# A hybrid decoder layer on one core: LayerNorm 1 rows normalised on another engine, and the last two blocks' sums in another order

## The chip, the cores and the metric

The kernel runs on one core of one Trainium2 chip. The metric is the device time of one execution in microseconds (us), lower is better. Engines are named as in the profile: PE (TensorE matmul), PEld (its weight load), DVE (VectorE), ACT (ScalarE), POOL (GpSimd), SP (SyncE, which here issues the DMAs).

## The reference, cut

One layer of a decoder trunk on a residual stream x of 1024 tokens by 1024 channels, in fp32:

```python
h = x * (1 + scale1) + shift1
y = concat(ssd_heads(h), attention_heads(h)) @ W_out
x = layer_norm(alpha * x + (1 + gate1) * y, g1, b1)      # LayerNorm 1
h = x * (1 + scale2) + shift2
x = layer_norm(alpha * x + (1 + gate2) * (relu(h @ W1)**2 @ W2), g2, b2)
```

The change lies at the seam in the middle: the last product of the mixer (`@ W_out`), LayerNorm 1, and the first products of the feed-forward part (`h @ W1`).

## The kernel before

Products of fp32 values are made as three products of split values: every operand is a high part (a cast to fp32r, mostly on ACT, L81) and a low part (raw minus high, mostly on DVE, L85), and PE adds high by high, high by low and low by high.

**The loop over token blocks.** The output projection runs over 8 blocks of 128 tokens (`for tb in range(TB)`, ending at L865). For a block, `out_mm` issues 24 products of 128x512 for each half of the channels, 48 in all; `y_rms` makes the RMS factor of the next block's rows (a product into `rms_ps`, DVE L628, POOL L629); L860 scales a half; and `norm` (L761 to L777) adds the residual (L767), takes the statistics (L768, L769), adds the epsilon (L770), takes the power on POOL (L771) and normalises the 128x1024 row block `u` on DVE (L777). For the last block the row is normalised in two halves, L774 on DVE and L775 on ACT, after a small DVE operation (L773) that makes the bias for ACT.

**To the feed-forward part.** `to_h2` of block tb is called one block later: PE transposes `u` in two halves of four (L813, into a PSUM tile `t_ps` of a tag "S" that has two buffers, shared with `rms_ps`), ACT copies the halves out with scale and bias (L820, four copies a half). The feed-forward products W1 are made in the way of Strassen and Winograd, with seven products of block sums of `h` and W1 instead of eight. Blocks 0 to 3 are split directly into the operands `h_hl`. For blocks 4 to 7 four sums of two token halves are made, t1, t3, t2 and t4 (L795), on POOL for blocks 4 and 5 and on DVE for 6 and 7, and their splits are the operands `h_s`. In the profile `u` is the row block, `h_t` the transposed half (and the tiles of t2 and t3), `h_f` the tiles of t1 and t4, `w_s` and `raw_w` block sums of W1 made on POOL (L792 adds, L795 subtracts), `w_op` their split parts.

**Behind the loop.** The first two column pairs of W1 run the two products that need only blocks 0 to 3 and the low halves (48 matmuls, `f_ps<-h_hl,w_op`, L961). Then their third operand's sums are made (`next(p.w)`), `to_h2` of the last block runs, the sums are split (`h_split` 5, 6, 4, 7), and the other five products follow in the order 5, 6, 4, 7, 3.

**What sets the order.** Each engine runs its instructions strictly in the order in which the build lays them down. The build's scheduler picks that order with a cost model of its own; the code's order and `issue_after` (the kernel's `after`) bound it. So a line that is moved in the code can move other engines' instructions past each other.

## Time and profile before

| | us |
|---|---|
| median of 3 timed runs | 1740.33 (1738.44 to 1745.25) |
| the profiled execution: its own time | 1742.31 |
| the profiled execution: span of the trace | 1740.6 |
| PE busy in the span | 1650.5 (95%) |
| DVE busy | 1235.1 (71%) |
| POOL busy | 820.7 (47%) |
| ACT busy | 763.8 (44%) |

The granted clock of PE is 0.98 over the whole span. The share of an engine is an average over many stages. The seam that the change touches is the stretch from 994 to 1126 us, and it is read from the timelines of the engines there: each row of a timeline has a start, a length, the engine, the line, the operation with its tiles, and in brackets how long the engine had been idle and what released it.

### The profile page before, as it was taken

Reading aid. Unit: us, or ns where it says so; the run is one execution under the profiler, and the core shown is the slowest. Engines: PE = TensorE matmul, PEld = TensorE weight load, DVE = VectorE, ACT = ScalarE, POOL = GpSimd, SP = SyncE. Lnnn points to the kernel's source line nnn. Section 1 sums busy time; section 2 is a strip of 40 time slices with the busy share of each in tenths; the row PEclk is TensorE's granted clock in tenths of the full one; section 3 lists DMA queues with packets and bytes.
Section 4 is the critical chain, followed back from the end, with each engine's and each line's share of the span. In section 5 each row is a group of like instructions: output and inputs, shape, how many; then the busy total and the mean of one; then the engine's idle time right before and its main releaser. Section 6 shows DMA issues by size and latency. Waiting matters only on the chain.

```text
span 1740.6 us, 22970 instructions
## 1 busy us (share of the span) xinstructions
PE 1650.5 (95%) x8316; PEld 1367.9 (79%) x8316; DVE 1235.1 (71%) x1889; ACT 763.8 (44%) x1372; POOL 820.7 (47%) x670
## 2 busy tenths in 40 slices
PE   8999899899999999999899999799999999999996
PEld 6777787788887878888778887688888878888885
DVE  6656677686787777676666378986767865746678
ACT  6557355414444444454565334633333334343322
POOL 4311222256566466354432455566656624705525
PEclk9999999999999999999999999899999999999998
DMA  8134343334444544433323644043444596666512
GB/s 331 37 124 146 109 145 110 121 130 158 154 139 175 165 142 164 138 129 123 121 95 123 228 157 170 37 174 135 146 140 161 172 345 208 250 243 205 193 37 97
DMA packets 112034, 268.73 MB, mean 154 GB/s; under 512 B 10129, under 2 KB 37009, under 8 KB 111921
## 3 DMA queue, kind: packets, MB, share of 16 engines
q1 hardware_dynamic: 111920, 267.27, 44.2%
q8 instruction: 65, 1.06, 0.2%
q14 instruction: 49, 0.39, 0.1%
HBM read 194.22 MB, written 64.62 MB: 149 GB/s over the span
## 4 chain that ended last, share of the span: by engine, by line
PE 63%; DVE 14%; ACT 7%; DMA 6%; POOL 5%; issue 4%; SPq 0%; DVEq 0%; ACTq 0%; POOLq 0%
PE mm_ps L62 20%; PE f_ps L961 15%; PE s_ps L1077 9%; PE y_ps L1077 7%; PE s_ps L62 5%; PE o_ps L62 4%; PE t_ps L550 3%; DVE ada_red L138 2%; DMA w_b<-in_w_dram 2%; ACT scores L421 2%; POOL w_b L186 2%; DMA raw_ada<-in_w_ada_dram 1%; DVE w_hl L85 1%; DVE conv_a L350 1%; POOL raw_ada L136 1%
## 5 line engine op out<-in xcount | busy, mean ns | idle before, releaser
L62 PE MATMUL mm_ps<-h_hl,w_hl 128*128 128x512 f32 x2016 | 506.4, 401 | 10.3 <-POOL w_hl L79 5.6
L62 PEld LDWEIGHTS mm_ps<-h_hl,w_hl 128*128 128x128 f32 x2016 | 375.1, 191 | 88.4 <-POOL w_hl L79 6.5
L85 DVE TENSOR_TENSOR w_op<-raw_w,w_op 128x512 fp32r<-128x512 f32 (+1 forms) x149 | 189.9, 1279 | 22.3 <-ACT w_op L81 21.7
L961 PE MATMUL f_ps<-h_s,w_op 128*128 128x512 f32 x768 | 183.6, 394 | 6.2 <-ACT h_s L81 3.0
L961 PEld LDWEIGHTS f_ps<-h_s,w_op 128*128 128x128 f32 x768 | 145.8, 190 | 38.1 <-ACT h_s L81 3.4
L528 POOL TENSOR_SCALAR probs<-probs,m 128x128 f32<-128x128 f32 (+7 forms) x128 | 103.3, 811 | 123.9 <-DVE m L527 121.7
L81 ACT CAST w_op<-raw_w 128x512 fp32r<-128x512 f32 (+1 forms) x149 | 114.6, 775 | 99.7 <-PE f_ps L961 53.1
L1077 PE MATMUL s_ps<-w_op,a_op 128*128 128x512 f32 x672 | 153.3, 389 | 1.1 <-DVE a_op L85 1.1
L1077 PEld LDWEIGHTS s_ps<-w_op,a_op 128*128 128x128 f32 x672 | 126.0, 188 | 27.8 <-DVE a_op L85 1.6
L85 DVE TENSOR_TENSOR a_op<-a_ld,a_op 128x1024 fp32r<-128x1024 f32 x53 | 79.1, 1494 | 92.3 <-ACT a_op L81 92.3
L526 ACT ACTIVATE probs<-probs,m 128x128 f32<-128x128 f32 (+7 forms) x128 | 99.2, 776 | 100.4 <-DVE m L525 91.1
L961 PE MATMUL f_ps<-h_hl,w_op 128*128 128x512 f32 x576 | 136.8, 389 | 0.0
L79 POOL TENSOR_SCALAR w_hl<-raw_w 128x512 fp32r<-128x512 f32 x86 | 58.8, 685 | 165.1 <-PE mm_ps L62 128.6
L136 POOL TENSOR_TENSOR raw_ada<-raw_ada,c_act 128x1024 f32<-128x1024 f32 x38 | 76.8, 2020 | 126.7 <-DMA raw_ada<-in_w_ada_dram 84.9
L85 DVE TENSOR_TENSOR w_hl<-raw_w,w_hl 128x512 fp32r<-128x512 f32 x88 | 85.5, 974 | 69.5 <-POOL w_hl L79 69.4
L552 ACT CAST pt_hl<-t_ps 128x512 fp32r<-128x512 f32 (+1 forms) x160 | 84.7, 541 | 100.4 <-PE t_ps L550 98.3
L81 ACT CAST a_op<-a_ld 128x1024 fp32r<-128x1024 f32 x53 | 55.7, 1054 | 159.6 <-PE s_ps L1077 80.5
L961 PEld LDWEIGHTS f_ps<-h_hl,w_op 128*128 128x128 f32 x576 | 108.1, 188 | 22.4
L62 PE MATMUL o_ps<-pt_hl,v_s 128*128 128x256 f32 (+1 forms) x640 | 108.9, 295 | 10.2 <-DVE pt_hl L553 4.0
L553 DVE TENSOR_TENSOR pt_hl<-t_ps,pt_hl 128x512 fp32r<-128x512 f32 (+1 forms) x160 | 99.7, 631 | 23.8 <-ACT pt_hl L552 22.3
L1077 PE MATMUL y_ps<-w_op,a_op 128*128 128x512 f32 x504 | 114.7, 389 | 0.0
L523 DVE CUSTOM_DVE_ANT_0 probs<-s_ps,cumrow 128x128 f32<-128x128 f32 (+7 forms) x128 | 94.7, 750 | 25.6 <-PE s_ps L62 18.0
(255 smaller groups left out, 3157.3 us busy)
## 6 DMA issues: line engine op xcount, KB each, us to landing
raw_w<-in_w_dram SPq DMA_DIRECT2D x57, 512.0 KB, 4.1
a_ld<-ad SPq DMA_DIRECT2D x49, 512.0 KB, 4.4
raw_ada<-in_w_ada_dram SPq DMA_DIRECT2D x48, 512.0 KB, 3.6
raw_w<-in_w_in_dram SPq DMA_DIRECT2D x44, 512.0 KB, 3.7
w_b<-in_w_dram SPq DMA_DIRECT2D x14, 1024.0 KB, 7.5
w2t<-w_b SPq DMA_DIRECT2D x14, 1024.0 KB, 4.3
ad<-a_s SPq DMA_DIRECT2D x28, 512.0 KB, 3.4
raw_w<-w2t SPq DMA_DIRECT2D x28, 512.0 KB, 4.8
```

The costliest lines, as they stand in the source:

```text
L62: nc.tensor.matmul(o, l, r, start=start, stop=stop)
L79: nc.gpsimd.tensor_scalar(hi, raw, 1.0, 1.0, op0=ALU.mult, op1=ALU.mult)
L81: nc.scalar.copy(hi, raw)
L85: eng.tensor_tensor(lo, raw, hi.bitcast(F32), op=ALU.subtract)
L136: nc.gpsimd.tensor_tensor(raw, raw, c_act.unsqueeze(2).broadcast_to([P, KT, P]), op=ALU.mult)
L523: nc.vector.tensor_tensor_reduce(out=pt, in0=sp[:, :W], in1=cum[:, :W], op0=ALU.add, op1=ALU.max, scale=1.0, scalar=-3.0e38, accum_out=m[: ...
L526: nc.scalar.activation(pt, pt, AF.Exp, bias=m[:, 1:2], scale=1.0, accum_out=m[:, 2:3])
L528: nc.gpsimd.tensor_scalar(pt, pt, m[:, 3:4], 1.0, op0=ALU.mult, op1=ALU.mult)
L552: nc.scalar.copy(hl[:, 0, :n], tp[:, :n])
L553: nc.vector.tensor_tensor(hl[:, 1, :n], tp[:, :n], hl[:, 0, :n].bitcast(F32), op=ALU.subtract)
L961: nc.tensor.matmul(o, l, r, start=first and k == 0 and m == 0, stop=last and k == 3 and m == 2, skip_group_check=True)
L1077: nc.tensor.matmul(banks[j], ahl[a_][:, n, js], whl[w_][:, n, :], start=first and d == 0 and n == 0 and m == 0, stop=last and d == ND - 1 ...
```

## The change

Three things are changed. First, the rows of LayerNorm 1 for blocks 0 to 6 are normalised by one ACT instruction (L779 of the changed kernel, `u * rstd + bias`), and a small POOL instruction (L778) makes the bias; for the last block the bias comes from POOL too (L773), while the two halves stay on DVE (L774) and ACT (L776). Second, the sums of blocks 4 to 7 are made in the order t1, t2, t4, t3 instead of t1, t3, t2, t4, with t1 right after the first half of the transposes; block 6's copies go to a tile of its own; and the sums of the last two blocks are drawn out between the `h_split` calls. Third, the third operand's sums of W1 for the first two column pairs are held behind the last block's power and DVE half (`after`).

```diff
-        nc.gpsimd.tensor_tensor(mv[:, 3:4], mv[:, 2:3], mhalf[:, 0:1], op=ALU.pow)
+        marks["pow"] = nc.gpsimd.tensor_tensor(mv[:, 3:4], mv[:, 2:3], mhalf[:, 0:1], op=ALU.pow)
         if last:
-            nc.vector.scalar_tensor_tensor(mv[:, 2:3], mv[:, 0:1], -1.0, mv[:, 3:4], op0=ALU.mult, op1=ALU.mult)
-            nc.vector.tensor_scalar(u[:, :512], u[:, :512], mv[:, 0:1], mv[:, 3:4], op0=ALU.subtract, op1=ALU.mult)
+            nc.gpsimd.tensor_scalar(mv[:, 2:3], mv[:, 0:1], mv[:, 3:4], -1.0, op0=ALU.mult, op1=ALU.mult)
+            marks["ln"] = nc.vector.tensor_scalar(u[:, :512], u[:, :512], mv[:, 0:1], mv[:, 3:4], op0=ALU.subtract,
+                                                  op1=ALU.mult)
             nc.scalar.activation(u[:, 512:], u[:, 512:], AF.Identity, bias=mv[:, 2:3], scale=mv[:, 3:4])
         else:
-            nc.vector.tensor_scalar(u, u, mv[:, 0:1], mv[:, 3:4], op0=ALU.subtract, op1=ALU.mult)
+            nc.gpsimd.tensor_scalar(mv[:, 2:3], mv[:, 0:1], mv[:, 3:4], -1.0, op0=ALU.mult, op1=ALU.mult)
+            nc.scalar.activation(u, u, AF.Identity, bias=mv[:, 2:3], scale=mv[:, 3:4])
...
     def to_h2(tb, u):
...
+        both = T4("pt", "h2_t", shape=(P, 2, 4, P)) if tb == TB - 2 else None
...
+            elif both is not None:
+                ht = both[:, hb]
...
+            if tb >= 4 and hb == 0:
+                sub(eng, hf[0][:, :, js], ht, hf[0][:, :, js])
         store(x2d[tb], u)
+        yield
+        if tb < 4:
+            return
+        b12, b22 = hts
+        t1, t4 = hf[0][:, :, js], hf[1][:, :, js]
+        sub(eng, t2f[:, :, js], b22, t1)
+        yield
+        sub(eng, t4, t4, t2f[:, :, js])
+        yield
+        sub(eng, t3f[:, :, js], b22, b12)
+        yield
+        parts(3, b22)
...
-        if before is not None:
-            to_h2(*before)
+        if before is not None and tb < TB - 1:
+            for _ in to_h2(*before):
+                pass
+        elif before is not None:
+
+            with after(marks["ln"]):
+                left = to_h2(*before)
+                next(left)
...
-    for p in first:
-        p.ready.append(next(p.w))
-    to_h2(*before)
+    with after(marks["ln"]), after(marks["pow"]):
+        for p in first:
+            p.ready.append(next(p.w))
+    left = [left, to_h2(*before)]
+    next(left[1])
...
     h_split(5, lambda k: hf[0][:, k, :], ["qk"] * 4)
+    for b in left:
+        next(b)
     h_split(6, lambda k: t2f[:, k, :], ["qk"] * 4)
+    for b in left:
+        next(b)
     h_split(4, lambda k: hf[1][:, k, :], ["v", "v", "w", "w"])
+    for b in left:
+        next(b)
+    for b in left:
+        next(b, None)
     h_split(7, lambda k: t3f[:, k, :], ["pt"] * 4)
```

Since the build lays the order down, what moved is read from the instructions of each engine. In the rows below `u_...` is the row block of one token block (the last one is `u_10002` before and `u_10009` after), `h_t_9242` is t3 and `h_t_9241` t2, and `w_s_10191` and `w_s_10199` before are `w_s_10190` and `w_s_10198` after. Line numbers of the changed kernel are higher by 2 (L795 becomes L797, L792 becomes L794), by 10 to 12 (L813 becomes L823, L820 becomes L832) or by 16 (L843, L844 and L860 become L859, L860 and L876).

POOL before, from the power of block 6 to just behind the power of block 7:

```order
L771 TENSOR_TENSOR mv<-mv,mhalf 128x1
L795 TENSOR_TENSOR w_s_10191<-raw_w 128x512
L792 TENSOR_TENSOR raw_w<-raw_w 128x512
L795 TENSOR_TENSOR h_t_9242<-h_t 128x4x128
L795 TENSOR_TENSOR h_t_9241<-h_t,h_f 128x4x128
L795 TENSOR_TENSOR raw_w<-raw_w 128x512
L795 TENSOR_TENSOR h_f<-h_f,h_t_9241 128x4x128
L795 TENSOR_TENSOR raw_w<-raw_w 128x512
L795 TENSOR_TENSOR w_s_10199<-raw_w 128x512
L792 TENSOR_TENSOR raw_w<-raw_w 128x512
L771 TENSOR_TENSOR mv<-mv,mhalf 128x1
L795 TENSOR_TENSOR raw_w<-raw_w 128x512 x2
```

POOL after, from the power of block 7:

```order
L771 TENSOR_TENSOR mv<-mv,mhalf 128x1
L797 TENSOR_TENSOR w_s_10190<-raw_w 128x512
L797 TENSOR_TENSOR w_s_10198<-raw_w 128x512
L773 TENSOR_SCALAR mv<-mv 128x1
L794 TENSOR_TENSOR raw_w<-raw_w 128x512 x2
L797 TENSOR_TENSOR raw_w<-raw_w 128x512 x4
L797 TENSOR_TENSOR w_s_10515<-raw_w 128x512
```

Before, two sums of W1 stand behind the last power; after, eight do, with the bias of the last block (L773) as the third instruction.

ACT before, from the copies of block 6 to the splits of the last block:

```order
L820 ACTIVATE h_t<-t_ps,b2t,g2t 128x128 x8
L81 CAST h_hl<-h_t 128x2x128 x2
L81 CAST w_op<-raw_w 128x512 x2
L775 ACTIVATE u_10002<-u_10002,mv 128x512
L81 CAST w_op<-raw_w 128x512
L81 CAST w_op<-w_s_10191 128x512
L820 ACTIVATE h_t<-t_ps,b2t,g2t 128x128 x8
L81 CAST h_hl<-h_t 128x2x128
```

ACT after, from the copies of block 5 to those of the last block:

```order
L832 ACTIVATE h_t<-t_ps,b2t,g2t 128x128 x4
L779 ACTIVATE u_9895<-u_9895,mv 128x1024
L832 ACTIVATE h_t<-t_ps,b2t,g2t 128x128 x4
L81 CAST h_hl<-h_t 128x2x128 x2
L81 CAST w_op<-raw_w 128x512
L832 ACTIVATE h_t<-t_ps,b2t,g2t 128x128 x8
L81 CAST h_hl<-h_t 128x2x128 x2
L776 ACTIVATE u_10009<-u_10009,mv 128x512
L81 CAST w_op<-raw_w 128x512 x4
L81 CAST w_op<-w_s_10190 128x512
L832 ACTIVATE h_t<-t_ps,b2t,g2t 128x128 x8
```

The normalisation of block 6 (`L779 u_9895`) stands between the two halves of block 5's copies, as it does for most blocks; and all the casts of W1's third operand (five) stand between the last block's normalisation and its copies, where three of the casts stood ahead of it before.

DVE before, from the last block's normalisation:

```order
L773 SCALAR_TENSOR_TENSOR mv<-mv 128x1
L774 TENSOR_SCALAR u_10002<-u_10002,mv 128x512
L85 TENSOR_TENSOR w_op<-raw_w,w_op 128x512 x3
L85 TENSOR_TENSOR w_op<-w_s_10191,w_op 128x512
L795 TENSOR_TENSOR h_f<-h_t,h_f 128x4x128
L795 TENSOR_TENSOR h_t_9242<-h_t 128x4x128
L795 TENSOR_TENSOR h_t_9241<-h_t,h_f 128x4x128
L85 TENSOR_TENSOR h_hl<-h_t,h_hl 128x2x128
L85 TENSOR_TENSOR h_s<-h_f,h_s 128x512 x2
L795 TENSOR_TENSOR h_f<-h_f,h_t_9241 128x4x128
```

DVE after, from the last block's normalisation:

```order
L774 TENSOR_SCALAR u_10009<-u_10009,mv 128x512
L797 TENSOR_TENSOR h_f<-h_t,h_f 128x4x128
L85 TENSOR_TENSOR h_hl<-h_t,h_hl 128x2x128 x2
L797 TENSOR_TENSOR h_t_9241<-h_t,h_f 128x4x128
L797 TENSOR_TENSOR h_f<-h_f,h_t_9241 128x4x128
L85 TENSOR_TENSOR w_op<-raw_w,w_op 128x512 x4
L85 TENSOR_TENSOR w_op<-w_s_10190,w_op 128x512
L797 TENSOR_TENSOR h_f<-h_t,h_f 128x4x128
L797 TENSOR_TENSOR h_t_9241<-h_t,h_f 128x4x128
L797 TENSOR_TENSOR h_t_9242<-h_t 128x4x128
L85 TENSOR_TENSOR h_hl<-h_t,h_hl 128x2x128
L797 TENSOR_TENSOR h_f<-h_f,h_t_9241 128x4x128
```

Before, only W1's four low parts stood between the last normalisation and the last block's t1; after, block 6's t1, t2 and t4, two of its splits and five low parts stand there. The order on PE and the order of SP's DMAs are the same but for a few matmuls' places.

## Rows read from the trace of the kernel before

**Rows 1.** The page's first part: busy us, share of the span, instructions.

```profile
PE 1650.5 (95%) x8316; PEld 1367.9 (79%) x8316; DVE 1235.1 (71%) x1889; ACT 763.8 (44%) x1372; POOL 820.7 (47%) x670
```

**Rows 2.** Busy us by stretch: PE, PEld, DVE, ACT, POOL (instructions); clock, DMA share, GB/s.

```profile
1065.00:1077.00 12.00, 10.02 (x50) 8.07 (x48) 11.54 (x14) 5.20 (x13) 6.41 (x5) 1.00 0.37 140
1077.00:1089.00 12.00, 10.76 (x53) 8.72 (x52) 11.18 (x14) 4.56 (x12) 9.98 (x7) 1.00 0.34 132
1089.00:1101.00 12.00, 12.00 (x59) 10.03 (x58) 11.20 (x14) 5.12 (x13) 11.24 (x10) 1.00 0.23 87
1101.00:1118.00 17.00, 7.39 (x29) 5.29 (x28) 15.85 (x21) 10.49 (x24) 9.74 (x7) 0.73 0.08 32
1118.00:1150.00 32.00, 32.00 (x132) 26.23 (x133) 28.70 (x43) 16.56 (x32) 10.58 (x8) 0.93 0.26 93
```

**Rows 3.** Timeline of PE, 1062 to 1122 us: start, length, operation, idle before.

```profile
1073.06 0.66 PE L813 MATMUL t_ps<-identf,u 128*128 128x128 f32 x4 [1.04 <-DVE r_rms L628]
...
1079.82 0.63 PE L813 MATMUL t_ps<-identf,u 128*128 128x128 f32 x4
...
1086.42 0.66 PE L813 MATMUL t_ps<-identf,u 128*128 128x128 f32 x4 [1.19 <-DVE r_rms L628]
...
1093.06 1.03 PE L813 MATMUL t_ps<-identf,u 128*128 128x128 f32 x8
1093.85 11.14 PE L961 MATMUL f_ps<-h_hl,w_op 128*128 128x512 f32 x48
1109.22 1.94 PE L813 MATMUL t_ps<-identf,u 128*128 128x128 f32 x8 [4.23 <-DVE u L774]
1114.15 1.22 PE L961 MATMUL f_ps<-h_s,w_op 128*128 128x512 f32 x2 [2.99 <-ACT h_s L81]
```

**Rows 4.** Timeline of PE, 1105 to 1160 us: where PE resumes.

```profile
1117.76 21.16 PE L961 MATMUL f_ps<-h_s,w_op 128*128 128x512 f32 x82 [2.39 <-DVE h_s L85]
```

**Rows 5.** Timeline of DVE, 1062 to 1120 us.

```profile
1065.41 0.81 DVE L777 TENSOR_SCALAR u<-u,mv 128x1024 f32<-128x1024 f32 x1 [0.73 <-POOL mv L771]
...
1090.52 1.77 DVE L777 TENSOR_SCALAR u<-u,mv 128x1024 f32<-128x1024 f32 x1 [0.67 <-POOL mv L771]
...
1104.40 0.14 DVE L770 TENSOR_SCALAR mv<-mv 128x1 f32<-128x1 f32 x1
1104.46 0.68 DVE L795 TENSOR_TENSOR h_t<-h_t,h_f 128x512 f32<-128x512 f32 x1
...
1105.73 1.75 DVE L795 TENSOR_TENSOR h_f<-h_f,h_t 128x512 f32<-128x512 f32 x1
...
1108.54 0.54 DVE L774 TENSOR_SCALAR u<-u,mv 128x512 f32<-128x512 f32 x1
...
1110.80 0.68 DVE L85 TENSOR_TENSOR w_op<-w_s,w_op 128x512 fp32r<-128x512 f32 x1
1111.92 0.69 DVE L795 TENSOR_TENSOR h_f<-h_t,h_f 128x512 f32<-128x512 f32 x1 [0.45 <-ACT h_t L820]
```

**Rows 6.** Timeline of POOL, 1062 to 1120 us.

```profile
1089.94 0.55 POOL L771 TENSOR_TENSOR mv<-mv,mhalf 128x1 f32<-128x1 f32 x1 [0.68 <-DVE mv L770]
...
1100.93 1.30 POOL L795 TENSOR_TENSOR w_s<-raw_w 128x512 f32<-128x512 f32 x1
...
1104.62 0.93 POOL L771 TENSOR_TENSOR mv<-mv,mhalf 128x1 f32<-128x1 f32 x1 [0.69 <-ACT w_op L81]
1105.52 3.08 POOL L795 TENSOR_TENSOR raw_w<-raw_w 128x512 f32<-128x512 f32 x2
```

**Rows 7.** Timeline of ACT, 1062 to 1120 us.

```profile
1071.23 1.06 ACT L619 ACTIVATE y_raw<-y_raw 128x1024 f32<-128x1024 f32 x1 [5.26 <-POOL y_hl L85]
...
1103.96 1.14 ACT L81 CAST w_op<-raw_w 128x512 fp32r<-128x512 f32 x2 [5.33 <-POOL raw_w L792]
1108.65 0.81 ACT L775 ACTIVATE u<-u,mv 128x512 f32<-128x512 f32 x1 [3.55 <-DVE mv L773]
...
1110.40 2.89 ACT L820 ACTIVATE h_t<-t_ps,b2t,g2t 128x128 f32<-128x128 f32 x8
```

More of the change, by code (lines that the diff above doesn't have):

```diff
@@ L807, in to_h2, with parts @@
         eng = nc.vector if tb >= TB - 2 else nc.gpsimd
+        both = T4("pt", "h2_t", shape=(P, 2, 4, P)) if tb == TB - 2 else None
         hts = []
+        def parts(o, ht):
+            for i in range(2):
+                t = hb_hl[o][i]
+                split(ht[:, 2 * i:2 * i + 2, :], t[:, :, 0, js], t[:, :, 1, js], "act")
         for hb in range(2):
@@ L822, in to_h2 @@
             hts.append(ht)
-            o = (1, 2)[hb] if tb < 4 else (None, 3)[hb]
-            if o:
-                for i in range(2):
-                    t = hb_hl[o][i]
-                    split(ht[:, 2 * i:2 * i + 2, :], t[:, :, 0, js], t[:, :, 1, js], "act")
-        if tb >= 4:
-            b12, b22 = hts
-            t1, t4 = hf[0][:, :, js], hf[1][:, :, js]
-            sub(eng, t1, b12, t1)
-            sub(eng, t3f[:, :, js], b22, b12)
-            sub(eng, t2f[:, :, js], b22, t1)
-            sub(eng, t4, t4, t2f[:, :, js])
-        store(x2d[tb], u)
+            if tb < 4:
+                parts(hb + 1, ht)
+            if tb >= 4 and hb == 0:
+                sub(eng, hf[0][:, :, js], ht, hf[0][:, :, js])
+        store(x2d[tb], u)
+        yield
+        if tb < 4:
+            return
[8 more added lines that the diff above has]
+        parts(3, b22)
     def u_pre(tb):
```

## The prediction

> **What bounds the kernel now.** I read the page's first part, then the busy time by stretch around the seam, then the timelines of the four engines there. On the page PE is busy for 1650.5 of 1740.6 us [rows 1], so only the stretches in which PE is idle can give time back. At the seam the stretches say where: PE works 10.02 and 10.76 of 12 us in the last blocks but one, all 12 from 1089 to 1101, 7.39 of 17 from 1101 to 1118, and then all 32 of the next 32 [rows 2]. The reader is to see that DVE is as full as PE in the loop (11.54, 11.18 and 11.20 of 12) and fuller behind it (15.85 of 17), while ACT has more than half of each loop stretch free.
>
> The timeline of PE puts places to this. In the loop PE waits 1.04 and 1.19 us before a second half of transposes, each time for DVE's RMS factor, which stands in DVE's queue [rows 3]. Behind the loop stand the 48 products without a gap, from 1093.85 to 1104.99, and then three waits: 4.23 us for the last block's normalised half (L774), 2.99 for the first split of t1, 2.39 for its low part; PE resumes for good at 1117.76 [rows 3, 4]. These 9.61 us are the large sum at the seam. What ends them is a chain: the last statistics end on DVE at 1104.54 [rows 5], the power on POOL at 1105.55 [rows 6], the last block's t1 starts at 1111.92 [rows 5], and PE resumes 5.84 us after that. So two numbers decide: when the last power is done, and what stands between it and that t1.
>
> **What two engines cost each other.** A DVE sum of 512 columns takes 0.68 us at 1104.46 and 1.75 at 1105.73, where POOL runs sums too; the 1024-wide normalisation takes 0.81 alone and 1.77 beside POOL [rows 5]. Two POOL sums take 3.08 us in that place [rows 6]. Taken as turns this adds up: two POOL sums of 1.24 and one DVE sum of 0.60 are 3.08. One POOL sum with little beside it is 1.30. I take turns as the rule here, 1.24 a POOL sum and 0.60 a DVE operation of 512 with two inputs from SBUF, and keep "no price at all" as the other end.
>
> The Trainium skill (SBUF — State Buffer, "Who interferes with whom") calls the port pair of VectorE and GpSimd an exclusive lock, held for a whole instruction, which a VectorE instruction with two SBUF inputs and a GpSimd one that reads SBUF both need; ScalarE waits for nobody. This speaks for the move of the normalisation to ACT and against the queueing of W1's sums beside the last blocks' sums; rows 5 and 6 agree with it (0.68 against 1.75 us). By the lock alone the tail below comes to the serial sum, 1121.5 for the last t1; by no lock to 1114.8.
>
> **Part 1, the normalisation on ACT.** It takes L777 off DVE, 0.81 to 1.77 us a block [rows 5], seven times. It adds to the chain a small POOL operation, which the trace of before does not show: between nothing and the 0.55 us of the power alone [rows 6], I take 0.4. The ACT instruction is bounded by 1.06 us (a 1024-wide one) and twice 0.81 (the 512-wide one) [rows 7]; I take 1.06. From power to normalised row it is then 1.5 us instead of 0.8 to 1.8, about the same. What changes is the queue: on ACT the normalisation of a block stands ahead of the copies of the previous block's second half, in order. PE's second half for block 5 ends near 1087.1 [rows 3] and its copies could start at once, but they now wait for block 6's power (1090.49) [rows 6] plus 1.5: till 1092.0, then 1.45 for four copies, half of the 2.89 for eight [rows 7]. Behind them wait the splits of that half on DVE, and behind these, in DVE's order, the scaling of the next half; PE's transposes of block 6 need the PSUM buffer that these copies free. Before, those transposes started at 1093.06. Played through with these lengths, block 5's transposes come 1.3 us later than before, its second half 1.6 later, and block 6's 2 to 4 later, so that the 48 products run from about 1097.4 to 1108.5. DVE's gain (1.77 for block 6) and its wait for the splits (about 1.4) nearly cancel: the last power ends at 1105.2 instead of 1105.55. So part 1 gives 0.3 us to the chain, between minus 1.5 and plus 1.5. That the products end 3.5 us later costs nothing as long as the chain behind the power is longer; if it were short, PE could not go on before 1108.5, still 9.3 us before the present 1117.76.
>
> **Part 2 and 3, what stands between the power and the last t1.** On POOL eight W1 sums now stand behind the power where two stood, with the last block's bias as the third instruction. On ACT all five casts of W1's third operand stand between the last normalisation and the last block's copies; the third raw cast needs the fifth of these eight sums. On DVE there stand eleven operations: L774, t1, t2, t4 of block 6, two splits (half as wide, 0.35 each), five low parts.
>
> The whole in turns: eight sums at 1.24 are 9.9, the bias 0.4, DVE 0.45 + 3 x 0.60 + 2 x 0.35 + 5 x 0.60 = 5.95; from 1105.2 that is 1121.5. The last t1 need not wait for the last three POOL sums, so at best with turns it is 3 x 1.24 less, 1117.7. I take 1119.5. Without any price of turns ACT's chain still holds: five sums and the bias, 6.6, to 1111.8; the last three casts 1.6 (two casts of 512 take 1.14); four copies 1.4 [rows 7]: 1114.8. Against 1111.92 before, the last t1 is later by 2.9 at the least, 9.6 at the most, 7.6 in my sum.
>
> **From t1 to PE's resumption** it was 5.84 us. Now t1, t2, t3, one split, t4 stand ahead of the first low part on DVE, 4 x 0.60 + 0.35 + 0.60 = 3.4, with up to two of POOL's sums between (2.5): 3.4 to 5.9, I take 5.4. So PE resumes at 1124.9, between 1118.2 and 1127.4: later by **7.1 us**, 0.4 at the least, 9.6 at the most. After that PE has no idle time that could take it back [rows 2]: the whole lands in the end. The clock is 0.73 in the stretch with the gaps and 0.93 behind it [rows 2]; PE waits before its resumption in both kernels, so I take that cost as equal, plus or minus 1.5. Of the block order itself (t2 and t4 ahead of t3, in the order in which the products ask) the gain is at most the 0.60 of one sum on DVE, inside the sum above.
>
> Against the profiled execution's own 1742.31 this gives 1749.4; it stood 1.98 above the median of 1740.33, so the forecast against the median is **1747.4**.
>
> **Rivals.** First, no price for turns: POOL and DVE run beside each other, and only ACT's chain is late. For it: the DVE sum at 1104.46 took no more than 0.68 with POOL's last power beside it [rows 5]; against it: that power took 0.93 instead of 0.55 [rows 6], and the next DVE sum 1.75. It gives plus 0.4 to plus 3: 1741 to 1743.4. Second, the change does what its parts could do on their own: DVE, freed of 1.77 us a block, sends the RMS factor earlier (1.04 and 1.19 gone), the last power comes 2 to 3 us earlier, and the 4.23 us gap goes; the 48 products then end at about 1102 and POOL's sums start early enough. 1.04 + 1.19 + 4.23 = 6.5, with 2 to 3 of the other waits: minus 6.5 to minus 9.5, 1731 to 1734. For it speaks DVE at 11.2 of 12 in the loop [rows 2]; against it that ACT's in-order copies hold the same PSUM buffers and that eight sums still follow the power. Third, worse, and on the far side of the bound: ACT's queue holds up the loop itself. If DVE waits for the splits behind L779 longer than the 1.77 that it gained, each block's power moves the next, about 1.4 a block over the last four: the power ends at 1109 to 1111 and the tail of 7.1 comes on top: plus 10 to plus 13, 1750.5 to 1753.5. It decides as soon as the wait is longer than the gain, and my two numbers (1.4 and 1.77) are close. That the build does not do what the change says is partly so: the last t1 was to come first behind the loop, and stands behind eleven DVE operations.
>
> **How the numbers follow.** 0.5% is 8.7 us, about what a measurement can tell from no change: faster means below 1731.6, slower above 1749.0. Forecast 0.55, with its own range 1744 to 1751; first rival 0.19; second 0.12, half of it below 1731.6; third 0.14. Of the forecast a third lies above 1749.0. So faster 0.06, slower 0.55 / 3 + 0.14 = 0.32, same 0.62. The range leaves out most of the second rival and the end of the third: 1737 to 1753.
>
> **What would show it.** Right: POOL's eight sums in a row behind the last power with lengths of 1.2 to 1.8; ACT's copies of the last block behind the cast of `w_s`; PE idle from about 1110 to 1124 but for the transposes; copies of a second half that wait for L779. Wrong: the last power before 1103 or after 1108; the last t1 before 1115; a PE gap behind the 48 products shorter than 10 us in all; or PE idle time behind the resumption that takes the delay back.

## The result, and the profile after

The changed kernel takes 1747.94 us (median of 20 runs, 1742.03 to 1753.39), the kernel before 1738.49 (20 runs, 1733.36 to 1745.25): a ratio of 1.0052, interval 1.0043 to 1.0062, some 9 us slower. The two profiled executions have spans of 1747.9 and 1740.6 us, 7.3 apart; each is one execution, 1.7 and 3.8 us above the median of its kernel, so they differ by 2.1 less than the medians do. The stretch ahead of the seam differs from execution to execution by a few us, so from here on places in the seam are counted from the loop's first product, the first matmul of `mm_ps<-wo_hi,y_hl` (at 994.10 us in the trace of before, at 993.32 in that of after). Counted so, PE resumes 7.67 us later than before (131.33 against 123.66), and the rest of the program behind that takes the same time (623.25 and 622.84).

By stretch, as in [rows 2] (PE, PEld, DVE, ACT, POOL with instruction counts, then PE's clock, DMA share, GB/s):

```profile
1077.00:1089.00 12.00, 10.20 (x50) 8.26 (x49) 10.05 (x13) 5.78 (x13) 8.76 (x8) 1.00 0.34 128
1089.00:1101.00 12.00, 11.09 (x53) 8.78 (x52) 10.02 (x12) 7.16 (x18) 6.21 (x6) 1.00 0.24 87
1101.00:1118.00 17.00, 7.70 (x38) 6.04 (x36) 16.39 (x16) 6.80 (x15) 14.32 (x10) 0.82 0.08 32
1118.00:1130.00 12.00, 6.57 (x17) 4.77 (x18) 11.90 (x18) 9.84 (x19) 2.92 (x2) 0.55 0.00 0
```

PE now also loses time from 1077 to 1101 (10.20 and 11.09 of 12), and a second stretch with little PE work has come, 1118 to 1130 with 6.57 of 12. POOL, which worked 9.74 of 17 from 1101 to 1118, works 14.32 of it.

The timeline of PE through the last blocks and the 48 products (start, length, operation, idle before and what ended it), and below it where PE resumes:

```profile
1081.03 0.66 PE L823 MATMUL t_ps<-identf,u 128*128 128x128 f32 x4 [0.61 <-ACT h_t L832]
...
1087.66 0.66 PE L823 MATMUL t_ps<-identf,u 128*128 128x128 f32 x4 [1.19 <-DVE r_rms L628]
...
1094.66 0.66 PE L823 MATMUL t_ps<-identf,u 128*128 128x128 f32 x4 [0.18 <-ACT u L779]
1096.05 0.66 PE L823 MATMUL t_ps<-identf,u 128*128 128x128 f32 x4 [0.73 <-ACT h_t L832]
1096.46 11.15 PE L983 MATMUL f_ps<-h_hl,w_op 128*128 128x512 f32 x48
1107.45 0.60 PE L823 MATMUL t_ps<-identf,u 128*128 128x128 f32 x4
1108.89 0.66 PE L823 MATMUL t_ps<-identf,u 128*128 128x128 f32 x4 [0.85 <-ACT u L776]
```

```profile
1120.21 1.22 PE L983 MATMUL f_ps<-h_s,w_op 128*128 128x512 f32 x2 [10.66 <-ACT h_s L81]
1124.65 20.88 PE L983 MATMUL f_ps<-h_s,w_op 128*128 128x512 f32 x82 [3.22 <-DVE h_s L85]
```

The 4.23 us wait for the last block's row [rows 3] has gone: the last transposes run at 1107.45 and 1108.89. In its place stands a wait of 10.66 us for the first split of t1, and 3.22 for its low part. In the loop there are new short waits, 0.61, 0.18 and 0.73, for ACT's copies and rows.

The timelines of DVE, POOL and ACT in the tail:

```profile
1096.32 2.77 DVE L85 TENSOR_TENSOR h_hl<-h_t,h_hl 128x256 fp32r<-128x256 f32 x2 [1.84 <-ACT h_hl L81]
...
1103.20 0.16 DVE L770 TENSOR_SCALAR mv<-mv 128x1 f32<-128x1 f32 x1
...
1104.40 1.51 DVE L774 TENSOR_SCALAR u<-u,mv 128x512 f32<-128x512 f32 x1 [0.44 <-POOL mv L771]
...
1108.20 1.75 DVE L797 TENSOR_TENSOR h_t<-h_t,h_f 128x512 f32<-128x512 f32 x1
...
1111.54 6.76 DVE L85 TENSOR_TENSOR w_op<-raw_w,w_op 128x512 fp32r<-128x512 f32 x4
1118.22 0.68 DVE L85 TENSOR_TENSOR w_op<-w_s,w_op 128x512 fp32r<-128x512 f32 x1
1118.83 0.68 DVE L797 TENSOR_TENSOR h_f<-h_t,h_f 128x512 f32<-128x512 f32 x1
```

```profile
1103.44 0.93 POOL L771 TENSOR_TENSOR mv<-mv,mhalf 128x1 f32<-128x1 f32 x1 [3.19 <-DVE mv L770]
1104.33 2.72 POOL L797 TENSOR_TENSOR w_s<-raw_w 128x512 f32<-128x512 f32 x2
1107.04 0.95 POOL L773 TENSOR_SCALAR mv<-mv 128x1 f32<-128x1 f32 x1
1107.95 3.12 POOL L794 TENSOR_TENSOR raw_w<-raw_w 128x512 f32<-128x512 f32 x2
1111.03 6.72 POOL L797 TENSOR_TENSOR raw_w<-raw_w 128x512 f32<-128x512 f32 x4
```

```profile
1093.36 1.24 ACT L779 ACTIVATE u<-u,mv 128x1024 f32<-128x1024 f32 x1 [8.03 <-POOL mv L778]
1094.51 1.49 ACT L832 ACTIVATE h_t<-t_ps,b2t,g2t 128x128 f32<-128x128 f32 x4
...
1112.77 1.14 ACT L81 CAST w_op<-raw_w 128x512 fp32r<-128x512 f32 x2 [1.05 <-POOL raw_w L797]
1113.82 0.61 ACT L81 CAST w_op<-w_s 128x512 fp32r<-128x512 f32 x1
1114.34 2.89 ACT L832 ACTIVATE h_t<-t_ps,b2t,g2t 128x128 f32<-128x128 f32 x8
```

The chain reads down these rows. The power ends at 1104.37. Behind it POOL makes its eight sums and the bias without a gap until 1117.75. DVE's four low parts take 6.76 us, 1.69 each, while POOL's last four sums take 6.72; the fifth low part, with POOL idle, takes 0.68, and the last block's t1 follows at once at 1118.83. In the ACT rows ACT is idle for 8.03 us ahead of the row of block 6 (it is released by the bias, which follows that block's power), and the second half of block 5's copies stands behind the row; DVE then waits 1.84 us for the casts that follow (the first DVE row).

### The profile page after: what moved, and what is told of

It reads as the page before. It is cut to its first block, busy times and chain, and to the rows that moved or that the text cites. A ratio compares the mean times of both kernels' runs of the same rounds, so it can differ in the third digit from the quotient of the medians.

```text
span 1747.9 us, 22975 instructions
## 1 busy us (share of the span) xinstructions
PE 1646.4 (94%) x8316; PEld 1360.6 (78%) x8316; DVE 1233.7 (71%) x1881; ACT 771.5 (44%) x1379; POOL 824.5 (47%) x678
## 3 DMA queue, kind: packets, MB, share of 16 engines
q8 instruction: 65, 1.06, 0.2%
## 4 chain that ended last, share of the span: by engine, by line
PE 62%; DVE 14%; DMA 7%; ACT 7%; POOL 5%; issue 5%; SPq 0%; DVEq 0%; ACTq 0%; POOLq 0%
PE mm_ps L62 20%; PE f_ps L983 15%; PE s_ps L1109 9%; PE y_ps L1109 7%; PE s_ps L62 5%; PE o_ps L62 3%; PE t_ps L550 2%; DVE ada_red L138 2%; DMA raw_ada<-in_w_ada_dram 2%; ACT scores L421 2%; DVE conv_a L350 1%; DMA w_b<-in_w_dram 1%; DVE w_hl L85 1%; DVE w_op L85 1%; POOL w_b L186 1%
## 5 line engine op out<-in xcount | busy, mean ns | idle before, releaser
L85 DVE TENSOR_TENSOR w_hl<-raw_w,w_hl 128x512 fp32r<-128x512 f32 x88 | 80.6, 918 | 68.3 <-POOL w_hl L79 68.2
```

Of the source, the lines that this page charges most:

```text
L85: eng.tensor_tensor(lo, raw, hi.bitcast(F32), op=ALU.subtract)
```

## The experiments

The first theory was the prediction's: the loop's delay is hidden and the tail behind the power makes the loss, because W1's sums were put there. Its rival was ACT's queue in the loop. Both turned out to be halves of the answer, and each half is smaller alone than the theory said. The table gives the places for all kernels, in us from the loop's first product; the tail is the time from the power's end to PE's resumption.

| kernel | rows on | W1's sums held | 48 products start | last power ends | tail | PE resumes | ratio to before |
|---|---|---|---|---|---|---|---|
| before | DVE | no | 99.75 | 111.45 | 12.21 | 123.66 | 1 |
| e3_actrow | ACT | no | 103.54 | 115.28 | 12.21 | 127.49 | 1.0026 |
| e1_nohold | ACT | no | 103.99 | 113.36 | 13.94 | 127.30 | 1.0021 |
| e2_holdonly | DVE | yes | 97.94 | 104.74 | 18.56 | 123.30 | 1.0004 |
| e4b_dverow | DVE | yes | 99.20 | 105.39 | 20.30 | 125.69 | 1.0013 |
| after | ACT | yes | 103.14 | 111.05 | 20.28 | 131.33 | 1.0052 |
| e5_halfsums | ACT | yes, six halved | 104.22 | 112.11 | 17.05 | 129.16 | 1.0029 |
| e6c_castsfirst | ACT, behind casts | yes | 96.93 | 100.64 | 20.97 | 121.61 | 0.9992 |
| e6d_castsfirst_nohold | ACT, behind casts | no | 96.94 | 105.86 | 14.93 | 120.79 | 0.9995 |

before, e2 and e3 have the old order of the block sums; the others have the new one. Two traces of one kernel (e7 below, taken twice) differ by 0.8 us in such places, so a difference below that is not read as an effect.

**The hold taken away (e1_nohold).**

```diff
-    with after(marks["ln"]), after(marks["pow"]):
-        for p in first:
-            p.ready.append(next(p.w))
+    for p in first:
+        p.ready.append(next(p.w))
```

> The changed kernel without the hold on W1's third operand sums (the two nested after calls around next(p.w) are taken away; all else as changed). Theory, the eight W1 sums behind the last power make the tail: only three of them stand behind it here, nine operations on DVE and three sums in turns after the power give the last block's t1 at about 1113.5 instead of 1118.83, PE resumes at 1118 to 1120 instead of 1124.65, and the time is 5 to 6.5 us below the changed kernel, plus 1 to plus 3 against the kernel before. Rival, the row normalisation in ACT's queue makes it: PE still resumes after 1123, the time stays within 2 us of the changed kernel.

Measured: 1743.34 us, ratio 1.0021 (1.0006 to 1.0036), 0.31 points or 5.4 us below the changed kernel, as the theory had it. The tail is shorter by 6.34 us, but the power comes 2.31 later, so PE resumes only 4.03 us ahead of the changed kernel and still 3.64 behind the kernel before, a little more than the 1 to 3 us that were allowed. The hold is not all of it.

**The hold alone (e2_holdonly).** The same `after` put into the kernel before.

```diff
-        nc.gpsimd.tensor_tensor(mv[:, 3:4], mv[:, 2:3], mhalf[:, 0:1], op=ALU.pow)
+        marks["pow"] = nc.gpsimd.tensor_tensor(mv[:, 3:4], mv[:, 2:3], mhalf[:, 0:1], op=ALU.pow)
...
-    for p in first:
-        p.ready.append(next(p.w))
+    with after(marks["ln"]), after(marks["pow"]):
+        for p in first:
+            p.ready.append(next(p.w))
```

> The kernel before with the hold alone: W1's third operand sums of the first two pairs are held behind the last block's power and DVE half; rows on DVE and the sums' order as before. Theory: eight sums behind the power again, the last t1 at 1117 to 1120, PE resumes at 1123 to 1126, the time is plus 5.5 to plus 8 us against the kernel before. Rival (ACT's queue): within 1.5 us of the kernel before, since ACT's order in the loop is as it was.

Measured: 1740.71 us, ratio 1.0004 (0.9988 to 1.002). The theory fails here. POOL's power and its last four sums, DVE's low parts and the last t1, and PE's resumption in the timelines of e2:

```profile
1096.83 0.93 POOL L771 TENSOR_TENSOR mv<-mv,mhalf 128x1 f32<-128x1 f32 x1 [4.91 <-DVE mv L770]
...
1103.16 6.45 POOL L795 TENSOR_TENSOR raw_w<-raw_w 128x512 f32<-128x512 f32 x4
```

```profile
1105.08 5.68 DVE L85 TENSOR_TENSOR w_op<-raw_w,w_op 128x512 fp32r<-128x512 f32 x4
...
1111.29 0.68 DVE L795 TENSOR_TENSOR h_f<-h_t,h_f 128x512 f32<-128x512 f32 x1
```

```profile
1116.32 21.55 PE L961 MATMUL f_ps<-h_s,w_op 128*128 128x512 f32 x82 [2.43 <-DVE h_s L85]
```

The tail grows by 6.35 us, as much as from e1 to the changed kernel (6.34), but the power ends 6.71 earlier. Between the powers of blocks 6 and 7, where it gains 4.90 of this, six sums of W1 are gone from POOL and one W1 low part from DVE, and DVE's operations are shorter: its first two block sums there took 1.72 and 1.66 us in the kernel before and take 0.68 each in e2, as fewer turns would have it. The other 1.81 us stand already at block 6's power, ahead of every sum that moved, and stay unexplained. Alone, the hold moves time from ahead of the power to behind it and changes nothing in the total.

**The rows on ACT alone (e3_actrow).**

```diff
-            nc.vector.tensor_scalar(u, u, mv[:, 0:1], mv[:, 3:4], op0=ALU.subtract, op1=ALU.mult)
+            nc.gpsimd.tensor_scalar(mv[:, 2:3], mv[:, 0:1], mv[:, 3:4], -1.0, op0=ALU.mult, op1=ALU.mult)
+            nc.scalar.activation(u, u, AF.Identity, bias=mv[:, 2:3], scale=mv[:, 3:4])
```

> The kernel before with the rows of blocks 0 to 6 normalised on ACT alone (bias on POOL); the sums' order and the places of W1's sums are as the scheduler then lays them, two of eight behind the last power. Theory: the transposes of blocks 5 and 6 come 1 to 2.5 us later and the 48 products start at about 1096.5 instead of 1093.85, but the last power ends at 1104 to 1105.5 and PE resumes within 1.5 us of 1117.76; the time is minus 1 to plus 2 us against before. Rival (ACT's queue): PE resumes 5 us or more later, plus 5 to plus 8 us.

Measured: 1744.04 us, ratio 1.0026 (1.0012 to 1.0039). The tail is the same to a hundredth (12.21), and the whole loss lies ahead of it: the 48 products 3.79 us later, the power 3.83, PE's resumption 3.83. The theory's "hidden" falls, and the rival's 5 to 8 us is too much. DVE and POOL in the timelines of e3:

```profile
1094.84 2.75 DVE L85 TENSOR_TENSOR h_hl<-h_t,h_hl 128x256 fp32r<-128x256 f32 x2 [1.85 <-ACT h_hl L81]
...
1113.10 0.69 DVE L796 TENSOR_TENSOR h_f<-h_t,h_f 128x512 f32<-128x512 f32 x1 [0.45 <-ACT h_t L821]
```

```profile
1105.79 0.93 POOL L771 TENSOR_TENSOR mv<-mv,mhalf 128x1 f32<-128x1 f32 x1 [0.69 <-ACT w_op L81]
```

DVE waits 1.85 us for the casts behind the row on ACT, in this kernel as in the changed one; the last statistics and the power come as much later as the loop does. And this is not the only such wait. From the loop's first product to the last power there are six in e3, 9.7 us in all (DVE's waits by what ended them: total, times, longest); the changed kernel has 9.3 us of them, the kernel before none:

```profile
DVE h_hl L85 <- ACT h_hl L81: 9.7, 6, 1.9
```

By stretch (columns as above), from the loop's first product to the start of the last power, first before, then e3:

```profile
994.10:1104.62 110.52, 106.69 (x505) 88.15 (x503) 91.78 (x121) 44.22 (x103) 67.05 (x49) 1.00 0.41 145
991.44:1105.79 114.35, 109.15 (x505) 88.63 (x503) 90.44 (x114) 51.12 (x110) 67.63 (x55) 0.99 0.40 140
```

Seven normalisations, 9.5 us, have left DVE, but its busy time falls by 1.34 us alone, because operations that stayed take longer (for example sixteen of its splits 11.6 us instead of 8.5, five low parts 7.5 instead of 5.4), and its idle time grows by 5.17. Together that is the 3.83. Why those operations take longer is not shown.

**Six of eight sums halved (e5_halfsums).**

```diff
-        add(nc.gpsimd, a21, a21, a22)
-        sub(nc.gpsimd, a11, a21, a11)
-        sub(nc.gpsimd, a12, a12, a11)
+        hw = slice(0, 2) if n < 2 else slice(0, 4)
+        add(nc.gpsimd, a21[:, hw], a21[:, hw], a22[:, hw])
+        sub(nc.gpsimd, a11[:, hw], a21[:, hw], a11[:, hw])
+        sub(nc.gpsimd, a12[:, hw], a12[:, hw], a11[:, hw])
```

> The changed kernel in which six of the eight W1 sums of the first two pairs are made over half of their columns (128x256); the other half of those sums is left out. Nothing else is changed, every wait stays. Theory of turns: six times 0.6 us less in the chain, so the low parts of W1 on DVE fall from 1.7 to about 1.1 us each, the last t1 starts at 1115 to 1116 instead of 1118.83, and the time is 3 to 4 us below the changed kernel. Rival, no price of turns, only ACT's chain of five sums: the low parts stay at their length, t1 moves by the three half sums in that chain, 1.8 us at most.

Measured: 1744.13 us, ratio 1.0029 (1.0014 to 1.0045), 0.23 points below the changed kernel's, or 4 us. DVE's four low parts and POOL's last four sums in its timelines:

```profile
1115.57 4.60 DVE L85 TENSOR_TENSOR w_op<-raw_w,w_op 128x512 fp32r<-128x512 f32 x4
```

```profile
1115.07 4.56 POOL L797 TENSOR_TENSOR raw_w<-raw_w 128x256 f32<-128x256 f32 x4
```

Nothing on DVE was changed, and its low parts fall from 1.69 to 1.15 us each, in step with POOL's halved sums (6.72 to 4.56 for four). The tail is shorter by 3.23 us, where a price of no turns allowed 1.8 (the power is 1.06 later in this trace, so PE resumes 2.17 earlier). That DVE's time follows the length of POOL's instruction shows the turns directly.

**The rows back on DVE (e4b_dverow).** The reverse of e3's edit, in the changed kernel.

```diff
-            nc.gpsimd.tensor_scalar(mv[:, 2:3], mv[:, 0:1], mv[:, 3:4], -1.0, op0=ALU.mult, op1=ALU.mult)
-            nc.scalar.activation(u, u, AF.Identity, bias=mv[:, 2:3], scale=mv[:, 3:4])
+            nc.vector.tensor_scalar(u, u, mv[:, 0:1], mv[:, 3:4], op0=ALU.subtract, op1=ALU.mult)
```

> The changed kernel with the rows of blocks 0 to 6 normalised on DVE again; the hold on W1's sums and the sums' order stay. First theory (the tail alone, the loop's delay is hidden): the last power moves by less than 1.5 us, PE resumes within 1.5 us of the changed kernel, so does the time. New theory (ACT's order makes the loop late, and the hold pays for its tail by an earlier power): counted from the first product of the loop, the 48 products start at 97 to 99 us instead of 103.1, the last power ends at 103.5 to 106 instead of 111.1, the tail from it to PE's resumption keeps its 18 to 20, PE resumes at 122 to 125.5 instead of 131.3; the time is 6 to 9 us below the changed kernel, minus 1 to plus 2 against before.

Measured: 1742.97 us, ratio 1.0013 (1.0003 to 1.0023). The power ends 5.66 us earlier, the tail is the same (20.30 and 20.28), PE resumes at 125.69, 5.64 earlier; by the ratios it is 0.39 points or 6.8 us below the changed kernel. So the power did what the new theory said, and the first theory, under which nothing was to move, falls. The start of the 48 products (99.20), the tail and PE's resumption lie 0.2 to 0.3 outside the ranges given. Against e2 (the old order of sums) the tail is 1.74 longer, with the ratio higher by 0.09 points, inside the intervals.

**The row behind the copies on ACT (e6c_castsfirst).** The changed kernel, with nothing changed in the code but the place of the row's instruction in ACT's queue (`mv` is returned by `norm`, `marks["cp"]` is the last cast). The build then lays some of DVE's splits and statistics a few places elsewhere, too.

```diff
-        norm(u, os_, last=tb == TB - 1)
-        if before is not None and tb < TB - 1:
-            for _ in to_h2(*before):
-                pass
+        mv = norm(u, os_, last=tb == TB - 1)
+        if tb < TB - 1:
+            if before is not None:
+                for _ in to_h2(*before):
+                    pass
+                with after(marks["cp"]):
+                    nc.scalar.activation(u, u, AF.Identity, bias=mv[:, 2:3], scale=mv[:, 3:4])
+            else:
+                nc.scalar.activation(u, u, AF.Identity, bias=mv[:, 2:3], scale=mv[:, 3:4])
```

> The changed kernel with one order changed on ACT: the row normalisation of a block is queued behind the copies and casts of the block before (to_h2 is called ahead of it, and an after on the last cast). New theory (it is the place in ACT's queue, not the move to ACT): the 48 products start at 97 to 99 us after the loop's first product instead of 103.1, the power ends at 103 to 106, PE resumes at 121.5 to 125; minus 6.5 to minus 9.5 us against the changed kernel. Rival, the longer way from power to row (bias on POOL, then ACT): the 48 products still start after 101, at most 3 us of gain. First theory (only the tail): within 1.5 us.

Measured: 1739.35 us, ratio 0.9992 (0.998 to 1.0003), 0.6 points or 10 us below the changed kernel, a little more than expected. In the timeline of ACT the copies and casts of block 5's second half now run before the row of block 6 (L884):

```profile
1082.81 1.51 ACT L832 ACTIVATE h_t<-t_ps,b2t,g2t 128x128 f32<-128x128 f32 x4 [2.54 <-PE t_ps L823]
1084.20 0.72 ACT L81 CAST h_hl<-h_t 128x256 fp32r<-128x256 f32 x2
1086.55 1.24 ACT L884 ACTIVATE u<-u,mv 128x1024 f32<-128x1024 f32 x1 [1.64 <-POOL mv L778]
```

The first DVE row below is the low part that waited 1.84 us in the changed kernel; it runs without a wait, and the power (first POOL row) ends at 100.64 from the loop's first product, 10.41 earlier and 2.4 ahead of the range given. The tail stays long, as the low parts and the bias (1.22) show:

```profile
1085.97 0.41 DVE L85 TENSOR_TENSOR h_hl<-h_t,h_hl 128x256 fp32r<-128x256 f32 x1
...
1101.87 5.70 DVE L85 TENSOR_TENSOR w_op<-raw_w,w_op 128x512 fp32r<-128x512 f32 x4
...
1108.09 0.68 DVE L797 TENSOR_TENSOR h_f<-h_t,h_f 128x512 f32<-128x512 f32 x1
```

```profile
1092.39 0.55 POOL L771 TENSOR_TENSOR mv<-mv,mhalf 128x1 f32<-128x1 f32 x1 [1.48 <-DVE mv L770]
...
1095.61 1.22 POOL L773 TENSOR_SCALAR mv<-mv 128x1 f32<-128x1 f32 x1
```

So it is the place in the queue that costs the loop, not the engine: the rows on ACT, in the right place, start the 48 products 2.82 us earlier than the kernel before.

**The hold taken away there (e6d_castsfirst_nohold).** e1's edit in e6c.

```diff
-    with after(marks["ln"]), after(marks["pow"]):
-        for p in first:
-            p.ready.append(next(p.w))
+    for p in first:
+        p.ready.append(next(p.w))
```

> The kernel of e6c without the hold: W1's sums stand where the scheduler puts them, five of eight ahead of the last power. With the loop no longer held up by ACT, this tells what the hold alone is worth. If it pays for its tail by an earlier power (new theory): the power ends 4 to 8 us later than in e6c (104 to 109 us after the loop's first product instead of 100.6), the tail behind it is 5 to 8 us shorter, and the time is within 2.5 us of e6c. If the hold is a plain loss: 4 us or more below e6c.

Measured: 1739.41 us, ratio 0.9995 (0.998 to 1.0011): the power 5.22 later, the tail 6.04 shorter, the time the same. DVE's last statistics, and POOL's last power with the sum ahead of it:

```profile
1090.69 0.15 DVE L770 TENSOR_SCALAR mv<-mv 128x1 f32<-128x1 f32 x1
```

```profile
1093.96 1.28 POOL L797 TENSOR_TENSOR w_s<-raw_w 128x512 f32<-128x512 f32 x1
1095.21 0.54 POOL L771 TENSOR_TENSOR mv<-mv,mhalf 128x1 f32<-128x1 f32 x1
```

The statistics end 100.95 us after the loop's first product, only 0.95 later than in e6c, but the power starts 4.37 behind them and without a wait of POOL: it stands in POOL's own queue behind sums that run without a gap. So some 4.3 of the 5.22 us that the hold gains here are a place in POOL's queue, and not turns on DVE; in the kernel before and in e2 the power follows its statistics within 0.1 us. In both loops that ACT does not hold up the hold gives ahead of the power about what it takes behind it; in the loop that ACT holds up (after against e1) it gave 2.31 and took 6.34.

**The queue between power and t1 (e7_lean, e8_lean_dverow, e10_lean_nohold).** Three casts of W1's third operand and their low parts are queued behind the split of the last block's t1 (`marks["h5lo"]` and `marks["h5hi"]` are the last instructions of `h_split(5, ...)`); e7 is e6c with it, e8 is e4b, e10 is e6d.

```diff
         add(nc.gpsimd, a21, a21, a22)
+        if n < 2:
+            yield 5, op(a21)
+            with after(marks["h5lo"]), after(marks["h5hi"]):
+                sub(nc.gpsimd, a11, a21, a11)
+                sub(nc.gpsimd, a12, a12, a11)
+                o6 = op(a11)
+            yield 6, o6
...
```

> The kernel of e6c in which three of the five casts of W1's third operand and their low parts are queued behind the split of the last block's t1 (an after on DVE and ACT); POOL's eight sums stay behind the power. If what stands between power and t1 sets the tail: last t1 1.5 to 3 us earlier, PE resumes 2 to 4 us earlier than in e6c, and the time is 2 to 4 us below e6c and below the kernel before. Rival: PE then waits for the sixth product's operands (a new gap of 2 us or more behind the first 24 products), and the time is that of e6c within 1.5 us.

> The kernel of e4b (rows on DVE) with the same three casts and low parts queued behind the split of the last block's t1. As for e7: 2 to 4 us below e4b if the queue between power and t1 sets the tail, within 1.5 us of e4b if PE waits for the sixth product's operands instead. Against e7 it tells what the rows on ACT are worth once the tail is equal: the new theory gives 0 to 2 us for ACT, since DVE is freed of seven instructions of 0.8 to 1.8 us.

> The kernel of e6d (rows on ACT behind the copies, no hold) with the three casts and low parts of W1's third operand queued behind the split of the last block's t1, as in e7. Three sums are behind the power, and seven operations on DVE instead of eleven: the last power stays at 104 to 107 us after the loop's first product, the tail to PE's resumption falls from 14.9 to 11.5 to 13.5, PE resumes at 117 to 119.5 instead of 120.8; 2 to 4 us below e6d. If the lows are wanted before the sixth product, PE gets a second gap and the time is that of e6d.

> The kernel of e7 a second time, beside e10: its gain over the kernel before was 0.14% with an interval of 0.04 to 0.25%. If it is real, it comes again: minus 1.5 to minus 4 us against the kernel before.

Measured: e7 1737.61 us, ratio 0.9986 (0.9975 to 0.9996), and the second time 1737.82, 0.999 (0.9975 to 1.0004); e8 1740.72, 0.9995 (0.9984 to 1.0006); e10 1736.26, 0.9981 (0.997 to 0.9992). Counted from the loop's first product, PE resumes at 119.73 in e7 (118.93 the second time), at 122.27 in e8, at 119.99 in e10, against 121.61, 125.69 and 120.79 without the edit. In e7 and e10 PE's gain is less than was expected (1.88 and 0.80 us, the latter no more than e7's two traces differ; the ratios give 1 and 2.4 us); e8 gained 3.42 (3.1 by the ratios), of which 1.42 came from an earlier power. Between e7 and e8 the ratios differ by 0.09 points, 1.6 us in favour of ACT, inside the 0 to 2 expected and inside the intervals. No second gap came: behind PE's resumption in e10 the products run on, 82 in a row.

```profile
1110.09 20.88 PE L1003 MATMUL f_ps<-h_s,w_op 128*128 128x512 f32 x82 [3.22 <-DVE h_s L85]
```

e10 is the fastest kernel of this study, 0.19% below the kernel before and 0.7% below the changed one, and its interval excludes no change; that of e7 does so in one of its two measurements. In e10 the last power starts 4.36 us behind its statistics, again for its place in POOL's queue; a kernel that queues it ahead of those sums was not run.

**Four sums behind the last block's t3 (e9_poolt3).** e7, with t3 of the last block made on POOL and the four later sums of W1 queued behind it.

```diff
-        sub(eng, t3f[:, :, js], b22, b12)
+        marks["t3"] = sub(nc.gpsimd if tb == TB - 1 else eng, t3f[:, :, js], b22, b12)
...
-            with after(marks["h5lo"]), after(marks["h5hi"]):
+            with after(marks["h5lo"]), after(marks["h5hi"]), after(marks["t3"]):
                 sub(nc.gpsimd, a11, a21, a11)
```

> The kernel of e7 with four of the eight W1 sums moved behind the last block's t3, which is made on POOL instead of DVE. If the turns of the two engines between power and t1 set the tail: four sums of 1.24 us less there, the last t1 3 to 5 us earlier than in e7, PE resumes at 115 to 117.5 instead of 119.7 us after the loop's first product. What it may lose again: PE waits for the sixth product's operand of W1, whose low part now stands behind all of the last block's splits on DVE, a gap of up to 4 us behind the first 24 products. Time 4 us below e7 at best, 1 us above it at worst.

Measured: 1743.09 us, ratio 1.0032 (1.0018 to 1.0046), 5 us above e7. PE starts on the low part of t1 at 1109.62, 119.06 from the loop's first product, 0.67 earlier than in e7 and no more than e7's two traces differ. The last t1 and the splits behind it on DVE:

```profile
1102.70 0.69 DVE L797 TENSOR_TENSOR h_f<-h_t,h_f 128x512 f32<-128x512 f32 x1 [1.03 <-ACT h_t L832]
...
1107.81 6.84 DVE L85 TENSOR_TENSOR h_s<-h_f,h_s 128x512 fp32r<-128x512 f32 x4
```

Counted from the power's end t1 starts 2.1 us sooner than in e7 (10.15 against 12.27), where 3 to 5 us in all had been expected, and the power is 1.41 later in this trace. The first row shows what holds it now: t1 waits 1.03 us for ACT's copies, where in e7 it followed two low parts without a pause. Behind it the four splits of t1 take 6.84 us (3.56 in e7), with the moved sums beside them on POOL. Then PE waits twice more, 2.65 us, ended by ACT's copy of an earlier product out of PSUM, and 4.07 us for W1's low part:

```profile
1109.62 6.90 PE L1003 MATMUL f_ps<-h_s,w_op 128*128 128x512 f32 x22 [3.96 <-DVE h_s L85]
1119.17 0.73 PE L1003 MATMUL f_ps<-h_s,w_op 128*128 128x512 f32 x2 [2.65 <-ACT f_e L1016]
1123.97 14.79 PE L1003 MATMUL f_ps<-h_s,w_op 128*128 128x512 f32 x58 [4.07 <-DVE w_op L85]
```

The gap that was feared, up to 4 us for the low part, came as 4.07; the 2.65 ahead of it was not foreseen. The sums have to stand somewhere between the power and the sixth product, and here they cost more.

## Why the prediction was right, and where its working was wrong

**The time and its sum.** 1747.4 was forecast, 1747.94 measured. The two are that near by luck: the forecast was 7.1 us above a median of 1740.33, of three runs, and the kernel before then measured 1738.49 beside the changed one, so the loss was 9.0 us by the ratio (7.5 to 10.8). In the profiled execution PE was to resume at 1124.9; it did at 1124.65 (7.1 against 6.89 us later on the clock of the two traces). The terms behind the power came out well in size: the last t1 was to start 14.3 us behind the power, it started 14.46 behind it (1104.37 to 1118.83); from t1 to PE's resumption 5.4 was taken, 5.82 measured. The 14.3 was a middle between all eight sums and three fewer, on the reason that t1 need not wait for the last three; it did come behind all eight, the serial sum of 16.3 us was 1.8 too long, and the bias took 0.95 instead of 0.4. The price of turns was the main choice, 1.24 for a POOL sum and 0.60 for a DVE operation: together 1.84 a pair, and four pairs took 6.72 to 6.76, 1.69 each. e5 shows that they are turns. The Trainium skill (SBUF — State Buffer, "Who interferes with whom") calls the port pair of VectorE and GpSimd an exclusive lock held for a whole instruction; the 1.69 us of a 0.68 us operation agrees with it.

**The step that failed: the loop's delay as a thing that costs nothing, and the power left in its place by a cancelling of DVE's gain and wait.** The power did come where it was said (1105.2 forecast, 1104.37 measured, 0.40 earlier than before when counted from the loop's first product), but for another reason. e3 shows that the rows on ACT alone make the power 3.83 us later, not 0.3 earlier: the working set one wait on the casts (1.4) against one normalisation (1.77), while the loop has six such waits, 9.7 us in all, and the time freed on DVE is mostly taken up by operations that got longer. e2 shows that the hold alone makes the power 6.71 earlier, a gain that the working did not have at all: it counted the six sums that arrived behind the power, and not what their leaving did ahead of it, on DVE by fewer turns (e2) or in POOL's own queue (e6d). The third rival had named this mechanism (ACT's queue holds up the loop) and its point, a wait longer than the gain; it was priced at plus 10 to plus 13 because the hold's gain was missing there too. In the sum the two errors were opposite, and the total came out right; that the power came where it was said was luck.

**What the loss is made of.** Neither part explains it alone: the rows give 0.26%, the hold 0.04%, both with the new order of sums 0.52%. Ahead of the power ACT's queue takes 3.8 us (e3), and it takes away what the hold should earn there: 2.31 us of an earlier power (e1 to after) instead of 6.71 (before to e2) or 5.22 (e6d to e6c). Behind the power the hold costs 6.0 to 6.4 us in each of these three pairs. One move in ACT's queue (e6c) removes the whole loss while the hold and its tail stay. How much of the loss is the two parts' joint effect is known roughly only: in PE's resumption the parts alone add up to 3.5 us of the 7.67, but they were measured in the old order of sums, and neither the new order alone nor both parts in the old one were run.

**The rivals.** "No price of turns" is refuted by e5. "The parts do what they could" has its loop half shown by e6c and e6d: with the row in the right place the 48 products start 2.8 us earlier than before; its size of 6.5 to 9.5 us was too much, the best version here gains 2.1 in the medians (e10, 1736.26 beside 1738.33) and 3.3 by its ratio. The waits of 1.04 and 1.19 us for the RMS factor did not go in the changed kernel: 1.16 and 1.19 stand there too (the latter in the PE rows above).

**The block sums' order** was put at 0.60 us at most. In e1 against e3 it makes the tail 1.73 longer and the power 1.92 earlier, with PE's resumption 0.19 earlier; in e4b against e2 the resumption is 2.39 later, and the intervals of the times overlap. What the order is worth by itself stays open within about 2.5 us.

**What the change was to show.** Eight sums in a row behind the power, copies of the last block behind the cast of `w_s`, copies of a second half behind the row, PE idle from about 1110 to 1124: all four are in the rows above. None of them could have told the two causes apart; only the kernels that undo one part each did.

## What to carry to other kernels

Work that is moved behind a point leaves a place ahead of it as well: size both sides, with each queue's turns and with what stands in line behind that work, before calling the move a gain or a loss. An instruction that waits for a late value must stand in its engine's queue behind the work that is ready, above all behind what frees buffers for another engine; where a scheduler lays the order, look at it and pin that one place. A right total is no evidence for its terms: undo each part alone, and both, since their prices need not add.

## What the runs showed of the hardware that was not expected

Small instructions, too, are longer where DVE and POOL both work. POOL's bias over 128x1 takes 0.27 to 0.41 us in the loop, 0.95 in the changed kernel's tail and 1.22 in e6c's (both in rows above), where the prediction took 0.4; the power takes 0.55 alone and 0.93 beside a DVE sum [rows 5, 6]. And the 1024-wide row on ACT takes 1.24 us, not the 1.06 of another 1024-wide instruction there [rows 7].
